# Buffers and products with v of an RWKV scan step, taken after the step before it

## The chip, the cores and the metric

One core of one Trainium2 chip. The time is the device time of one execution in microseconds (us); the kernel before was run three times. The trace is of one more execution, taken with the profiler.

## The reference, cut to what matters

A two-layer encoder on 256 tokens of width 1024. Each layer is a half feed-forward block, a mixer of three branches, and a second half feed-forward block; every block is scaled and shifted by rows that are products of the conditioning vector with `ada_w`. The mixer:

```python
o_a = dilated_attention(...); o_b = neighborhood_attention(...)
o_c = rwkv7_bidirectional(...)
merged = (sigmoid(gz0) * (o_a @ w_branch[0]) + sigmoid(gz1) * (o_b @ w_branch[1])
          + sigmoid(gz2) * (o_c @ w_branch[2]))
return merged @ w_out
```

and in `rwkv7_bidirectional`, over 256 tokens, 8 heads of 64, two directions:

```python
sa = einsum("dbhvk,dbhk->dbhv", state, a_vec)
state = state * w[..., None, :] + sa[..., None] * b_vec[..., None, :] + v[..., None] * k[..., None, :]
y = einsum("dbhvk,dbhk->dbhv", state, r)
```

## The kernel before, in words

**Dense work.** Weights are read once, in order, in tiles of 128x1024 f32 (`wraw`), split into a high part on ScalarE (`whi`, L360) and a low part on VectorE (`wlo`, L369), and used on TensorE in threes of matmuls (L404 to L406), one three for each 128x128 weight tile. In what follows a "dense three" is such a three. Four split quarters and three raw tiles may be held at once. In a mixer the dense work is: projections for the scan, for attention A and B, then branch A with its gates, the gates of branch C (tile `sg2`, two buffers), branch B with its gates, and at last branch C, whose input `oC` is what the scan leaves; then `w_out`.

**The scan in chunks.** The 256 steps of the recurrence are four chunks of 64 tokens, for both directions at once (chunk n of the one direction with chunk 3-n of the other). `invert` makes for a chunk the products `pG` (tile G, two buffers, L1161), a first inverse of 8x8 blocks (`blocks8`: many small VectorE steps on `w`, one TensorE product with `b8`), and three rounds of `pX`, a copy, `pT`, a masked copy into `TT` and a transpose (`flip`, L1245). There are two such threads, for chunks 0 and 2 and for 1 and 3. `values` makes the transposes `pBT` (tile `bu`), the product `pvt` of v (tile `uv`) and `pMV` (tile `W1`), and runs beside the three rounds. `scan` goes through the four chunks one after another: `pAS` added to W1, `pU`, the new state `pS1`, the output `pY`. `post` then normalises (`pvar`, `pgi`) and leaves `oC`.

**Buffers.** Most tiles lie in 34 equal buffers (`big`; semaphore `s_big`). `invert` takes at its start all that a chunk needs: two for G, one each for `uv`, `bu` and `tw` (and one for `tx` per thread), and no more than two chunks may hold theirs (`s_ck`). The scan gives them back when it has ended the chunk. The loads of `ada_w` (`araw`, 512 KB each, 72 a layer, L495; each used by one VectorE instruction, L468) take a buffer each from the same 34, and so do the gates `sg2` and much of attention.

**Order.** All of it is written by threads of Python generators. A planner (`Order`) gives each step an estimated duration, keeps a clock for each engine, and lets the thread go on that can start first; what comes out is the order of the instructions in each engine's queue. On the chip each queue runs in that order, and an instruction that waits holds all behind it in its queue. So a thread that may start earlier or later in the plan moves instructions in all queues.

Of the kernel before, what the change touches and what calls it, by code (L numbers as in the profile page):

```python
# [24 lines left out]
NBIG, NZ, NZ2 = 34, 10, 2  # L25
NRAW, NSPL, NADA, NPM = 3, 4, 2, 3
ORDER = "cabAgB"
NCK, NLR = 2, 2
WARM = 0
NJ0 = 8  # L30
NXF, NXM = 4, 8
# [4 lines left out]
VPRIO = 4  # L36
# [125 lines left out]
def wait(ev):  # L162
    return ("wait", ev, 0, 0)
# [6 lines left out]
def take(sem, n=1):  # L170
    return ("take", sem, n, 0)
# [20 lines left out]
def trunk(ctx, tc, A, out):  # L192
# [9 lines left out]
    od = Order()  # L202
    s_raw, s_spl, s_ada = Sem(NRAW), Sem(NSPL), Sem(NADA)
    s_pm, s_px, s_big = Sem(NPM), Sem(8 - NPM), Sem(NBIG)
# [9 lines left out]
    def big(name, shape=(128, 4, S), dt=F32):  # L214
        return act.tile(list(shape), dt, name=name, tag="b4", bufs=NBIG)
# [7 lines left out]
    def free_big(n=1):  # L223
        od.release(s_big, n)
# [597 lines left out]
    def half(h):  # L822
        return slice(64 * (h % 2), 64 * (h % 2) + 64)
# [29 lines left out]
    def mixer(l, st):  # L853
# [268 lines left out]

        e_inv, e_val = ([Event() for _ in range(4)] for _ in range(2))
        CH = {}
        s_ck = Sem(NCK)
        n_inv, e_got = [0], [Event() for _ in range(5)]

        def toks(c):
            return slice(c * 64, c * 64 + 64)
# [1 line left out]
        def invert(ns):  # L1131
            for e in e_ab:
                yield wait(e)
            for n in ns:
                cs = (n, 3 - n)
                if n > 0:
                    yield wait(e_got[n - 1])
                yield take(s_ck)
                for _ in range(5 - (n == 3) + (n == ns[0])):
                    yield take(s_big)  # L1140
                od.set(e_got[n])
                if n == ns[0]:
                    tx = big("tx", (128, 2, 2, 4, 64))
                    T, X = tx[:, 0], tx[:, 1]
                G = [big("G", (128, 2, 4, 128)) for _ in range(2)]
                uv = big("uv", (128, 2, 8, 64))
                bu = big("bu", (128, 2, 8, 64)) if n < 3 else None
                tw = big("tw", (128, 2, 2, 4, 64))
                TT, W1 = tw[:, 0], tw[:, 1]
                for d in range(2):  # L1150
                    yield take(s_px, 2)
                    pp = [paux("pG", (128, 4, 128)) for _ in range(2)]
                    yield on("PE", 1.3)
                    for i in range(4):
                        for b in range(2):
                            hs = half(b)
                            P.matmul(pp[b][:, i], BK[d][i // 2][hs, i % 2, cs[d]].rearrange("p a b -> p (a b)"),
                                     ar_view(d, i // 2)[hs, :, i % 2, toks(cs[d])], start=True, stop=True)
                    for b in range(2):
                        yield on("DVE", 0.6)  # L1160
                        V.tensor_mul(G[b][:, d], pp[b], mg[:, d][:, None, :].to_broadcast([128, 4, 128]))  # L1161
                        od.release(s_px)
                yield from blocks8(G, X, TT)
                yield on("DVE", 0.6)
                flip(T, TT)
                od.spawn(values(n, cs, G, bu, uv, W1), VPRIO)
                for lv in range(3):
                    w = 8 << lv

                    def part_(t, d, a):  # L1170
                        return t[:, d].rearrange("p h c -> p (h c)").rearrange("p (x a s) -> p x a s", a=2, s=w)[:, :, a]

                    def halves_(t, a):
                        return skew(part_(t, 0, a), part_(t, 1, 1 - a))

                    yield take(s_px)
                    px = paux("pX", (128, 2, 4, 64))
                    yield on("PE", 0.85)
                    for d in range(2):
                        for h in range(8):  # L1180
                            P.matmul(px[half(h), d, h // 2], G[h % 2][half(h), d, h // 2, 0:64], T[half(h), d, h // 2],  # L1181
                                     start=True, stop=True)
                    if lv == 0:
                        yield from copy_any(X, px, 512)
                    else:
                        yield from copy_any(halves_(X, 0), halves_(px, 0), 256)
                    od.release(s_px)
                    yield take(s_px)
                    pt = paux("pT", (128, 2, 4, 64))
                    yield on("PE", 0.85)  # L1190
                    for d in range(2):
                        for h in range(8):
                            P.matmul(pt[half(h), d, h // 2], X[half(h), d, h // 2], TT[half(h), d, h // 2], start=True, stop=True)  # L1193
                    yield on("DVE", 0.335)
                    V.copy_predicated(halves_(TT, 1), lvl[:, lv].rearrange("p d (x s) -> p d x s", s=w), halves_(pt, 1))
                    od.release(s_px)
                    if lv < 2:
                        yield on("DVE", 0.6)
                        flip(T, TT)
                CH[n] = (G, bu, uv, TT, W1)  # L1200
                yield wait(e_val[n])
                od.set(e_inv[n])
            n_inv[0] += 1
            free_big(1 if n_inv[0] == 1 else 5)

        def blocks8(G, m, TT):

# [36 lines left out]

            V.transpose(t.rearrange("p d a b -> p (d a b)"), tt.rearrange("p d a b -> p (d a b)"))  # L1245

        def values(n, cs, G, bu, uv, W1):
            for d in range(2):
                yield wait(e_rkv[d, 2])
            if n < 3:  # L1250
                yield take(s_px, 2)
                p = [paux("pBT", (128, 2, 4, 64)) for _ in range(2)]
                yield on("PE", 0.9)
                for d in range(2):
                    for i in range(4):
                        for b in range(2):
                            hs = half(b)
                            P.transpose(p[b][:, d, i], BK[d][i // 2][hs, i % 2, cs[d]].rearrange("p a b -> p (a b)"), ident[hs, hs])
                for b in range(2):
                    yield from copy_any(bu[:, :, b:8:2], p[b], 512)  # L1260
                    od.release(s_px)
# [17 lines left out]
            yield from copy_any(W1, p, 512)  # L1279
            od.release(s_px)  # L1280
            od.set(e_val[n])

        e_y = {(d, t): Event() for d in range(2) for t in range(2)}

        def scan():
            ST = st2 = None
            yield wait(e_ab[0])
            yield take(s_big)
            for n in range(4):
                cs = (n, 3 - n)  # L1290
                yield wait(e_inv[n])
                G, bu, uv, TT, W1 = CH[n]
                ar = lambda d, h, z: ar_view(d, h // 4)[half(h), z, h // 2 % 2, toks(cs[d])]
                dh = [(d, h) for d in range(2) for h in range(8)]
                if ST is None:
                    st2 = big("st", (128, 2, 2, 4, 64))
# [49 lines left out]
                od.release(s_px)  # L1346
                free_big(5 - (n == 3))
                od.release(s_ck)
                ST = sn
            free_big(5)  # L1350

# [566 lines left out]
```

## Time and profile before

| | |
|---|---|
| median of three runs | 1579.02 us (1576.25 to 1579.44) |
| profiled execution | 1579.55 us, span of its trace 1577.7 us |
| PE (matmul) busy | 1509.2 us, 96% of the span |
| PEld (weight load) busy | 1440.4 us, 91% |
| DVE busy | 1288.8 us, 82% |
| ACT busy | 856.1 us, 54% |
| DMA, mean | 197 GB/s |

PE is the engine with the most work. The shares are over the whole program; the mixers of the two layers (about 210 to 615 us and 980 to 1385 us) are where it has stretches without work. The granted TensorE clock is 1.00 (2.4 GHz) nearly everywhere and 0.50 (1.2 GHz) in a few stretches of the mixers.

### The profile page before, as it was taken

The numbers are of one execution on the slowest core, as the hardware profiler recorded it, in microseconds if no ns is written. First come the engines' busy times: TensorE is split into PE (matmuls) and PEld (weight loads), VectorE is DVE, ScalarE is ACT, GpSimd is POOL, SyncE is SP. The second block draws the span as 40 slices with busy tenths as digits, with TensorE's granted clock in tenths as the row PEclk, the third lists the DMA queues.
The fourth block names the chain that finished last, engine by engine and source line by source line (L and its number), as shares of the span: only waits on it lengthen the run. The fifth ranks groups of instructions, "written<-read, shape, count | busy, mean of one in ns | idle before, by whom it ended". The sixth has DMA issues, their size and how long they took to land.

```text
span 1577.7 us, 36363 instructions
## 1 busy us (share of the span) xinstructions
PE 1509.2 (96%) x14470; PEld 1440.4 (91%) x14470; DVE 1288.8 (82%) x2732; ACT 856.1 (54%) x1730; POOL 2.3 (0%) x22
## 2 busy tenths in 40 slices
PE   6999999999899989999999999999999987999997
PEld 6998999979689879999999999998888977999997
DVE  8888789989768688988789877999897687998664
ACT  4556457566344347555565545676654433665554
POOL 0000000000000000000000000000000000000000
PEclk9999999999899969999999999999999988999999
DMA  9687864446223435887668885543652352457553
GB/s 345 215 301 269 277 224 162 163 147 234 100 95 133 135 139 196 274 289 262 221 208 278 276 273 195 189 159 129 219 165 100 122 190 106 146 202 267 188 187 121
DMA packets 96226, 311.58 MB, mean 197 GB/s; under 512 B 11444, under 2 KB 22964, under 8 KB 96056
## 3 DMA queue, kind: packets, MB, share of 16 engines
q1 hardware_dynamic: 95768, 309.15, 57.8%
q8 instruction: 113, 1.85, 0.5%
q14 instruction: 57, 0.47, 0.1%
q10 hardware_dynamic: 288, 0.10, 0.0%
HBM read 308.17 MB, written 1.05 MB: 196 GB/s over the span
## 4 chain that ended last, share of the span: by engine, by line
PE 88%; DVE 6%; DMA 3%; issue 1%; ACT 1%; SPq 1%; DVEq 0%; ACTq 0%
PE pmain L404 21%; PE pmain L405 20%; PE pmain L406 20%; DMA araw<-in_ada_w_dram 3%; PE pearly L404 2%; PE pearly L406 2%; PE pearly L405 2%; PE pX L1181 1%; DVE araw L468 1%; PE pT L1193 1%; PE pS L1499 1%; PE pfirst L405 1%; PE pfirst L406 1%; PE pfirst L404 1%; DVE wlo L369 1%
## 5 line engine op out<-in xcount | busy, mean ns | idle before, releaser
L360 ACT CAST whi<-wraw 128x512 fp32r<-128x512 f32 x828 | 508.5, 619 | 444.6 <-PE pmain L405 291.8
L369 DVE TENSOR_TENSOR wlo<-wraw,whi 128x512 fp32r<-128x512 f32 x828 | 566.6, 689 | 118.0 <-ACT whi L360 108.0
L404 PE MATMUL pmain<-h,whi 128*128 128x256 f32 x1840 | 528.1, 287 | 0.0
L405 PE MATMUL pmain<-h,whi 128*128 128x256 f32 x1840 | 517.4, 281 | 0.0
L406 PE MATMUL pmain<-h,wlo 128*128 128x256 f32 x1840 | 515.6, 280 | 0.0
L404 PEld LDWEIGHTS pmain<-h,whi 128*128 128x128 f32 x1840 | 346.1, 188 | 12.2 <-issue 8.2
L406 PEld LDWEIGHTS pmain<-h,wlo 128*128 128x128 f32 x1840 | 347.4, 189 | 0.3 <-DVE wlo L369 0.2
L405 PEld LDWEIGHTS pmain<-h,whi 128*128 128x128 f32 x1840 | 346.4, 188 | 1.1 <-issue 0.7
L468 DVE CUSTOM_DVE_ANT_0 araw<-araw,csb 128x1024 f32<-128x1024 f32 x144 | 174.7, 1218 | 47.1 <-DMA araw<-in_ada_w_dram 46.9
L406 PE MATMUL pmain<-z,wlo 128*128 128x256 f32 x704 | 198.5, 282 | 7.0 <-DVE wlo L369 7.0
L405 PE MATMUL pmain<-z,whi 128*128 128x256 f32 x704 | 198.4, 282 | 0.0
L404 PE MATMUL pmain<-z,whi 128*128 128x256 f32 x704 | 197.7, 281 | 0.0
L406 PEld LDWEIGHTS pmain<-z,wlo 128*128 128x128 f32 x704 | 132.8, 189 | 8.5 <-DVE wlo L369 8.4
L404 PEld LDWEIGHTS pmain<-z,whi 128*128 128x128 f32 x704 | 132.7, 189 | 0.0
L405 PEld LDWEIGHTS pmain<-z,whi 128*128 128x128 f32 x704 | 132.7, 188 | 0.0
L404 PE MATMUL pearly<-xh,whi 128*128 128x258 f32 x320 | 91.5, 286 | 0.0
L406 PE MATMUL pearly<-xh,wlo 128*128 128x258 f32 x320 | 90.4, 283 | 0.0
L405 PE MATMUL pearly<-xl,whi 128*128 128x258 f32 x320 | 90.1, 282 | 0.0
L405 PEld LDWEIGHTS pearly<-xl,whi 128*128 128x128 f32 x320 | 60.6, 189 | 0.0
L404 PEld LDWEIGHTS pearly<-xh,whi 128*128 128x128 f32 x320 | 60.6, 189 | 0.0
L406 PEld LDWEIGHTS pearly<-xh,wlo 128*128 128x128 f32 x320 | 60.4, 189 | 0.0
L427 ACT CAST z<-ffz 128x256 fp32r<-128x256 f32 x76 | 30.6, 405 | 35.2 <-DVE ffz L659 34.8
(301 smaller groups left out, 2369.8 us busy)
## 6 DMA issues: line engine op xcount, KB each, us to landing
wraw<-in_ffn_wi_dram SPq DMA_DIRECT2D x160, 512.0 KB, 4.6
araw<-in_ada_w_dram SPq DMA_DIRECT2D x144, 512.0 KB, 6.4
wraw<-in_ffn_wo_dram SPq DMA_DIRECT2D x88, 512.0 KB, 4.6
wraw<-in_w_in_dram SPq DMA_DIRECT2D x78, 512.0 KB, 4.0
wraw<-in_w_gb_dram SPq DMA_DIRECT2D x72, 512.0 KB, 3.8
w0raw<-in_ffn_wi_dram SPq DMA_DIRECT2D x16, 512.0 KB, 11.1
wraw<-in_w_out_dram SPq DMA_DIRECT2D x16, 512.0 KB, 3.7
bt<-in_bt_dram SPq DMA_DIRECT2D x16, 192.0 KB, 4.7
```

The costliest lines, as they stand in the source:

```text
L360: S_.copy(hi, part(q))
L369: V.tensor_tensor(lo, part(q), hi, op=OP.subtract)
L404: P.matmul(o, w[0], xh, start=first, stop=False)
L405: P.matmul(o, w[0], xl, start=False, stop=False)
L406: P.matmul(o, w[1], xh, start=False, stop=last)
L427: S_.copy(self.hi(k), src)
L468: V.tensor_tensor_reduce(out=raw, in0=raw, in1=csb, scale=0.5, scalar=0.0, op0=OP.mult, op1=OP.add, accum_out=modT[l][:, blk:blk + 1])
L1181: P.matmul(px[half(h), d, h // 2], G[h % 2][half(h), d, h // 2, 0:64], T[half(h), d, h // 2], start=True, stop=True)
L1193: P.matmul(pt[half(h), d, h // 2], X[half(h), d, h // 2], TT[half(h), d, h // 2], start=True, stop=True)
L1499: P.matmul(pS[e][:, t], qT[half(e), hp, t * 128:(t + 1) * 128], kT[half(e), hp], start=True, stop=True)
```

## The change

`invert` takes three buffers a chunk instead of five and no longer waits for `values` at its end. `values` takes `uv` and `bu` itself, in the order of the chunks, and only one chunk may hold them (`s_vl` is one): the scan gives it back when it has ended a chunk. So `pBT`, `pvt` and `pMV` of chunk n are made after the scan of chunk n-1, and the scan waits for both events.

```diff
@@ -25,7 +25,7 @@
 NBIG, NZ, NZ2 = 34, 10, 2
 NRAW, NSPL, NADA, NPM = 3, 4, 2, 3
 ORDER = "cabAgB"
-NCK, NLR = 2, 2
+NCK, NLR, NVL = 2, 2, 1
 WARM = 0
 NJ0 = 8
 NXF, NXM = 4, 8
@@ -1122,8 +1122,8 @@
 
         e_inv, e_val = ([Event() for _ in range(4)] for _ in range(2))
         CH = {}
-        s_ck = Sem(NCK)
-        n_inv, e_got = [0], [Event() for _ in range(5)]
+        s_ck, s_vl = Sem(NCK), Sem(NVL)
+        n_inv, n_val, e_got, e_vgot = [0], [0], *([Event() for _ in range(5)] for _ in range(2))
 
         def toks(c):
             return slice(c * 64, c * 64 + 64)
@@ -1136,15 +1136,13 @@
                 if n > 0:
                     yield wait(e_got[n - 1])
                 yield take(s_ck)
-                for _ in range(5 - (n == 3) + (n == ns[0])):
+                for _ in range(3 + (n == ns[0])):
                     yield take(s_big)
                 od.set(e_got[n])
                 if n == ns[0]:
                     tx = big("tx", (128, 2, 2, 4, 64))
                     T, X = tx[:, 0], tx[:, 1]
                 G = [big("G", (128, 2, 4, 128)) for _ in range(2)]
-                uv = big("uv", (128, 2, 8, 64))
-                bu = big("bu", (128, 2, 8, 64)) if n < 3 else None
                 tw = big("tw", (128, 2, 2, 4, 64))
                 TT, W1 = tw[:, 0], tw[:, 1]
                 for d in range(2):
@@ -1163,7 +1161,7 @@
                 yield from blocks8(G, X, TT)
                 yield on("DVE", 0.6)
                 flip(T, TT)
-                od.spawn(values(n, cs, G, bu, uv, W1), VPRIO)
+                od.spawn(values(n, cs, G, TT, W1), VPRIO)
                 for lv in range(3):
                     w = 8 << lv
 
@@ -1197,11 +1195,8 @@
                     if lv < 2:
                         yield on("DVE", 0.6)
                         flip(T, TT)
-                CH[n] = (G, bu, uv, TT, W1)
-                yield wait(e_val[n])
                 od.set(e_inv[n])
-            n_inv[0] += 1
-            free_big(1 if n_inv[0] == 1 else 5)
+            free_big()
 
         def blocks8(G, m, TT):
 
@@ -1244,9 +1239,18 @@
 
             V.transpose(t.rearrange("p d a b -> p (d a b)"), tt.rearrange("p d a b -> p (d a b)"))
 
-        def values(n, cs, G, bu, uv, W1):
+        def values(n, cs, G, TT, W1):
             for d in range(2):
                 yield wait(e_rkv[d, 2])
+            if n > 0:
+                yield wait(e_vgot[n - 1])
+            yield take(s_vl)
+            for _ in range(1 + (n < 3)):
+                yield take(s_big)
+            od.set(e_vgot[n])
+            uv = big("uv", (128, 2, 8, 64))
+            bu = big("bu", (128, 2, 8, 64)) if n < 3 else None
+            CH[n] = (G, bu, uv, TT, W1)
             if n < 3:
                 yield take(s_px, 2)
                 p = [paux("pBT", (128, 2, 4, 64)) for _ in range(2)]
@@ -1279,6 +1283,9 @@
             yield from copy_any(W1, p, 512)
             od.release(s_px)
             od.set(e_val[n])
+            n_val[0] += 1
+            if n_val[0] == 4:
+                free_big(4)
 
         e_y = {(d, t): Event() for d in range(2) for t in range(2)}
 
@@ -1288,6 +1295,7 @@
             yield take(s_big)
             for n in range(4):
                 cs = (n, 3 - n)
+                yield wait(e_val[n])
                 yield wait(e_inv[n])
                 G, bu, uv, TT, W1 = CH[n]
                 ar = lambda d, h, z: ar_view(d, h // 4)[half(h), z, h // 2 % 2, toks(cs[d])]
@@ -1346,6 +1354,7 @@
                 od.release(s_px)
                 free_big(5 - (n == 3))
                 od.release(s_ck)
+                od.release(s_vl)
                 ST = sn
             free_big(5)
 
```

What this does to the queues is shown at three places.

**TensorE where branch C begins, layer 0.** `o` is the output of attention B, `oC` that of the scan. Before:

```order
L404 MATMUL pmain<-o,whi 128x256
L405 MATMUL pmain<-o,whi 128x256
L406 MATMUL pmain<-o,wlo 128x256
L1337 MATMUL pY<-G,uv 64x64 x16
L1341 MATMUL pY<-ar,st 64x64 x16
L1302 MATMUL pAS<-st,ar 64x64 x16
L1310 MATMUL pU<-tw 64x64 x16
L1337 MATMUL pY<-G,uv 64x64 x16
L1341 MATMUL pY<-ar,st 64x64 x16
L1402 MATMUL pvar<-c_sel,gsq 128x2 x8
L1420 MATMUL pgi<-c_ident,gsq 128x128 x8
L404 MATMUL pmain<-oC,whi 128x256
```

With the change:

```order
L404 MATMUL pmain<-o,whi 128x256
L405 MATMUL pmain<-o,whi 128x256
L406 MATMUL pmain<-o,wlo 128x256
L404 MATMUL pmain<-oC,whi 128x256
L405 MATMUL pmain<-oC,whi 128x256
L406 MATMUL pmain<-oC,wlo 128x256
```

The scan's last steps no longer stand between the two: the last `pgi` of layer 0 is now 35 dense threes ahead of the end of branch B. In layer 1 the products that stood there (two whole inversions, two `pvt`, two `pMV`, two steps of the scan) are gone too but for one last `pgi` directly ahead of branch C; the last `pY` stands 26 dense threes ahead.

**VectorE in the first inversion, layer 0.** `w_` with a number is the small tile of one chunk's 8x8 blocks. Before, the second chunk's begins after the scan's first `uv` copy (L1312):

```order
L369 TENSOR_TENSOR wlo<-wraw,whi 128x512
L1195 COPY_PREDICATED tw<-lvl,pT 128x2x4x32
L1161 TENSOR_TENSOR G<-pG,c_mg 128x512 x2
L1312 COPY uv<-pU 64x8x64
L1161 TENSOR_TENSOR G<-pG,c_mg 128x512 x2
L1215 TENSOR_TENSOR tx<-G,c_m_112 64x512 x2
L1218 COPY w_5657<-c_d_113 128x64
L1219 TENSOR_REDUCE w_5657<-tx 128x64
```

With the change it runs between the steps of the first chunk's:

```order
L1228 TENSOR_TENSOR w_5233<-p_5288,w_5233 128x8x4
L1210 TENSOR_TENSOR tx<-G,c_m_112 64x512
L1232 TENSOR_TENSOR w_5233<-w_5233 128x2x4x4
L1210 TENSOR_TENSOR tx<-G,c_m_112 64x512
L1228 TENSOR_TENSOR w_5233<-p_5288,w_5233 128x8x3
L1213 COPY w_5334<-c_d_113 128x64
L1214 TENSOR_REDUCE w_5334<-tx 128x64
L1232 TENSOR_TENSOR w_5233<-w_5233 128x2x4x3
```

The 8x8 blocks of the second inversion have moved ahead of the 207th split `wlo` of the program, into the time in which branch A is done and the gates of branch C wait for buffers.

**The queue of loads (SP), end of the mixer of layer 1.** `w_gb` holds the gates and branches, `w_out` comes after branch C. Before:

```order
L495 DMA araw<-in_ada_w_dram 128x1024 x2
L345 DMA wraw<-in_w_gb_dram 128x1024 x5
L495 DMA araw<-in_ada_w_dram 128x1024
L345 DMA wraw<-in_w_out_dram 128x1024
L495 DMA araw<-in_ada_w_dram 128x1024 x12
L345 DMA wraw<-in_w_out_dram 128x1024 x7
```

With the change:

```order
L495 DMA araw<-in_ada_w_dram 128x1024 x2
L345 DMA wraw<-in_w_gb_dram 128x1024
L495 DMA araw<-in_ada_w_dram 128x1024
L345 DMA wraw<-in_w_gb_dram 128x1024 x2
L495 DMA araw<-in_ada_w_dram 128x1024 x2
L345 DMA wraw<-in_w_gb_dram 128x1024 x8
L345 DMA wraw<-in_w_out_dram 128x1024 x8
```

The twelve `ada_w` loads that were behind the first `w_out` tile have moved ahead of the last eight `w_gb` tiles. In layer 0 eight moved likewise, and eight now follow each other where three did, near the first inversion.

## Rows read from the trace of the kernel before

**Rows 1.** The page's part 1, TensorE's line alone.

```profile
PE 1509.2 (96%) x14470; PEld 1440.4 (91%) x14470; DVE 1288.8 (82%) x2732; ACT 856.1 (54%) x1730; POOL 2.3 (0%) x22
```

**Rows 2.** Busy time by stretch, layer 0: stall, interleaved part, tail, and slow-clock parts.

```profile
core 0: us, PE busy (x) PEld busy (x) DVE busy (x) ACT busy (x) POOL busy (x), PEclk, DMA share, GB/s
401.10:445.20 44.10, 35.18 (x504) 28.13 (x504) 33.42 (x86) 15.70 (x40) 0.00 (x0) 0.88 0.25 83
405.80:416.03 10.23, 8.98 (x32) 5.89 (x34) 8.76 (x32) 1.68 (x3) 0.00 (x0) 0.50 0.53 198
445.20:544.70 99.50, 99.14 (x1596) 93.00 (x1594) 71.83 (x158) 44.90 (x85) 0.00 (x0) 1.00 0.37 123
544.70:576.46 31.76, 21.05 (x245) 18.84 (x244) 23.10 (x51) 8.35 (x18) 0.00 (x0) 0.62 0.40 150
552.57:576.46 23.89, 16.54 (x114) 14.81 (x115) 18.12 (x41) 7.08 (x15) 0.00 (x0) 0.50 0.32 130
```

**Rows 3.** The same view, layer 1: stall, interleaved part, tail, and slow-clock parts.

```profile
1176.40:1195.70 19.30, 14.89 (x386) 13.40 (x385) 11.57 (x20) 5.32 (x10) 0.00 (x0) 1.00 0.44 146
1195.70:1290.80 95.10, 94.19 (x1094) 86.58 (x1092) 72.46 (x159) 46.12 (x99) 0.00 (x0) 1.00 0.37 123
1291.00:1347.87 56.87, 41.72 (x864) 36.97 (x864) 43.45 (x104) 15.56 (x32) 0.00 (x0) 0.79 0.37 140
1293.26:1303.50 10.24, 7.10 (x96) 5.32 (x98) 9.57 (x30) 1.66 (x3) 0.00 (x0) 0.50 1.01 381
1330.81:1334.22 3.41, 3.22 (x54) 3.10 (x56) 0.00 (x0) 0.14 (x1) 0.00 (x0) 0.50 0.00 0
1337.64:1347.87 10.23, 7.86 (x31) 6.63 (x32) 7.32 (x20) 3.21 (x9) 0.00 (x0) 0.50 0.01 2
```

**Rows 4.** Timeline, tail of layer 0: start us, duration us, what [idle before <-releaser].

```profile
546.63 5.35 SPq L495 DMA_DIRECT2D araw<-in_ada_w_dram  x8
...
569.71 0.58 PE L404 MATMUL pmain<-oC,whi 128*128 128x256 f32 x1 [3.73 <-ACT oC L1447]
```

**Rows 5.** Timeline, stall of layer 0.

```profile
401.95 0.69 DVE L369 TENSOR_TENSOR wlo<-wraw,whi 128x512 fp32r<-128x512 f32 x1
...
407.05 2.08 PE L1228 MATMUL p<-tx,c_b 128*128 128x512 f32 x2 [5.21 <-DVE tx L1222]
...
409.16 0.22 DVE L1233 TENSOR_TENSOR w<-p,w 128x56 f32<-128x56 f32 x1 [0.49 <-PE p L1228]
...
415.83 0.17 DVE L1237 TENSOR_TENSOR w<-w 128x8 f32<-128x8 f32 x1
...
432.30 0.69 DVE L369 TENSOR_TENSOR wlo<-wraw,whi 128x512 fp32r<-128x512 f32 x1 [2.71 <-ACT whi L360]
```

**Rows 6.** Groups of instructions by line on VectorE: busy us, mean ns | idle before.

```profile
L468 DVE CUSTOM_DVE_ANT_0 araw<-araw,csb 128x1024 f32<-128x1024 f32 x144 | 174.7, 1218 | 47.1 <-DMA araw<-in_ada_w_dram 46.9
...
L1161 DVE TENSOR_TENSOR G<-pG,c_mg 128x512 f32<-128x512 f32 x32 | 21.1, 683 | 2.8 <-PE pG L1157 2.7
...
L1245 DVE STREAM_TRANSPOSE tx<-tw 128x512 f32<-128x512 f32 x24 | 16.9, 707 | 0.3
L1215 DVE TENSOR_TENSOR tx<-G,c_m 64x512 f32<-64x512 f32 x16 | 10.9, 682 | 0.2
L1219 DVE TENSOR_REDUCE w<-tx 128x64 f32<-128x512 f32 x8 | 9.2, 1151 | 0.0
```

**Rows 7.** Busy time by stretch where two inversions run at once, end of layer 1's mixer.

```profile
1280.00:1320.00 40.00, 30.42 (x580) 27.06 (x578) 38.17 (x92) 11.56 (x21) 0.00 (x0) 0.87 0.65 238
```

**Rows 8.** Answer for the tile araw from 380 to 620 us: its loads.

```profile
DMA to landing us min/median/max: 4.9/6.2/8.1
```

**Rows 9.** Answers for the tiles pvt, pMV and pBT: copies of their results (ns min/median/max).

```profile
L849 ACT COPY uv<-pvt x16: 578/580/582, 428.5 to 1321.9; 64x512 f32<-64x512 f32 x16
...
L849 ACT COPY tw<-pMV x8: 585/586/588, 430.9 to 1326.9; 128x512 f32<-128x512 f32 x8
...
L849 ACT COPY bu<-pBT x12: 585/589/595, 419.9 to 1302.0; 128x512 f32<-128x512 f32 x12
```

**Rows 10.** The chain that ended last, 450 to 500 us: products at the full clock.

```profile
456.56 0.65 PE pBT L1258 x16
...
470.15 1.08 PE pAS L1302 x32
...
481.98 1.09 PE pG L1157 x16
```

## The prediction

> **What bounds the kernel now.** I read the page's busy shares first. TensorE (PE) is busy 96% of the span [rows 1], and the change neither adds nor removes a matmul, so it can only give back time in which PE has nothing to do or runs at half clock. For that I cut the mixers by the view of busy time by stretch, at the points where PE's queue goes from dense threes to other work and back. What a stretch loses I count as its length, less PE's busy time, plus half of what PE did while the granted clock stood at 0.50, that is at 1.2 GHz where 2.4 is the full rate. The reader should see six numbers.
>
> Layer 0 [rows 2]: the stall after branch A loses 44.10 - 35.18 + 8.98/2 = 13.4 us; the interleaved part up to the end of branch B loses 0.4; the tail loses 31.76 - 21.05 + 16.54/2 = 19.0. Layer 1 [rows 3]: the stall loses 4.4, the interleaved part 0.9, the tail 56.87 - 41.72 + (7.10 + 3.22 + 7.86)/2 = 24.2. Together 62.3 us, of which the two tails are 43.2.
>
> In a tail the dense work that needs no scan has run out, and branch C waits: the timeline has its first matmul at 569.71, released by the copy to oC [rows 4]. The tail is the scan's chain, alone. The stall of layer 0 is another thing: PE waits there for VectorE (5.21 us at 407.05 for the blocks' tx) [rows 5], which is busy 33.42 of 44.10 us [rows 2]. So VectorE, with its dependences, is what a longer stall would be made of.
>
> **The change, part by part.** The instructions stay the same in kind and number; each term is a move.
>
> *The tails.* In the changed order the last pgi of layer 0 stands 35 dense threes ahead of the end of branch B. I take the tail of layer 0 as gone: -19.0 us, half-clock start of branch C included, since PE comes to it busy. In layer 1 the last pgi stands directly ahead of branch C, so what follows it remains: two VectorE products, the copy to oC and the low part. The row that is nearest is the 3.73 us that PE waited for just that chain in layer 0 [rows 4], at half clock and with one ada instruction in between. I take 3, with ends 0 and 8 (twice the row, if VectorE is behind). So layer 1 gives 24.2 - 3 = 21.2.
>
> *Stall of layer 0.* Between the 206th and 207th split (401.95 to 432.30) [rows 5] VectorE's queue gets the second chunk's start: four G, two tx, one reduction, 14 small steps of about 0.2, a transpose and three more ada instructions, against a few attention and bonus steps that move behind. By their durations [rows 5, 6] that is 4 x 0.68 + 2 x 0.68 + 1.15 + 14 x 0.2 + 0.71 + 3 x 1.22 = 12.4, less about 3: some 10 us more VectorE work, while PE gets 4.6 more work in the stretch (two pG of 1.09, a block product of about 1, one more pX and pT of 1.08, less what moved out; [rows 5, 10]). VectorE would then need 33.4 + 10 = 43.4 us. At its present share, 76%, that is 57 us against a PE work of 44.1 - 13.4 + 4.6 = 35.3: 22 lost. At 100%: 8 lost. The nearest row is the end of layer 1's mixer, where two inversions do run at once: VectorE is busy 38.17 of 40 us there, 95% [rows 7]. At 90% the stretch takes 48 and loses 13. I take no change, with ends -5 and +9.
>
> In the same place eight ada loads now follow each other in SP's queue, some behind buffers that VectorE or the last attention product gives back. A load takes 6.2 us to land, up to 8.1 [rows 8]; VectorE comes to the one that is issued last about 5 us after its buffer is free, so it waits 1 us or 2, inside the ends above. The w_gb tile behind them in SP's queue is for the 211th split, more than 10 us of VectorE's work later, so it hides. The Trainium skill, DMA: Bandwidth & Descriptors, Anatomy of one DMA, gives 2.0 us plus bytes over 436 GB/s, measured for loads that GpSimd issues; for 512 KB my estimate from it is 3.2 us, and the sum would be better by the 1 or 2 us; the trace's 6.2 differs from it and decides.
>
> *Interleaved part of layer 0.* From the 206th to the 222nd split VectorE's queue goes from about 48 to about 80 us: ten more ada, eight G, four tx, two reductions, some twenty small steps, three transposes, and the first post steps, by their durations [rows 5, 6] about 32 us. PE's work up to the same dense threes goes from about 60 to about 80. So two full queues with dependences between them stand where PE lost 0.4 us before. Here the change puts values on the scan's path: for each later chunk pvt (1.08, as the like product has), two copies of 0.58, pMV, a copy of 0.59 [rows 9, 10], ahead of them pBT of 0.65 and two copies. PE cannot pass them; what covers them is dense threes (two to five between each, 0.7 to 1.8 us) and the other inversion. If the cover is right they cost nothing, and if not each gap is lost at once. I take +5, ends 0 and +12.
>
> *Stall of layer 1.* VectorE gets about 13 us more between its splits, PE 7.5 us more; attention B's second half now lies in it. PE's work is 14.9 + 7.5 = 22.4; VectorE's 11.6 + 13 = 24.6, at 90% 27 us, and its attention chain adds some: +4, ends 0 and +10. The clock stayed at 1.00 through this stall [rows 3], and fell to 0.50 in that of layer 0 [rows 2]; were it to fall here as there, the price is half of 8.98 us, and the upper end holds it. The Trainium skill, TensorE: Matmul & The Clock Gate, HAM oscillation, says that waits for operands throw the clock back again and again; by it this fall would come and the sum would be about 4 us worse, and the trace shows it in one of two stalls.
>
> *Interleaved part of layer 1.* As in layer 0 but with less moved (VectorE 38 to 67, PE to 73 us): +3, ends 0 and +8.
>
> *The sum.* -19.0 - 21.2 + 0 + 5 + 4 + 3 = -28.2. The profiled execution took 1579.55 us (span 1577.7): 1551.3. It lies 0.5 above the median of the runs, so I say **1551 us**. Nothing outside the mixers changes its order.
>
> **The rivals.**
>
> *Full cover.* The two inversions fill each other's waits and the values are hidden: nothing is paid but 3 us of layer 1's tail, and the stall of layer 0 wins 3: about 1536. For it: 0.4 and 0.9 lost where scan and dense work are interleaved now [rows 2, 3]. Against it: VectorE has 72 of 99 us busy there, and gets more. Chance 0.2.
>
> *VectorE becomes the bound early.* The stall of layer 0 goes at 76% (+9), the interleaved parts and the stall of layer 1 near their upper ends (+8, +6, +4): -40 + 27 = -13, about 1566. For it: the 5.21 us wait [rows 5]. Against: the 95% where two inversions run [rows 7]. Chance 0.18.
>
> *Slower: the scan's path becomes the bound.* In six scan steps values now stand between one step and the next. Each is 1.08 + 0.58 + 0.58 + 1.08 + 0.59 = 3.9 us, four of them with 1.8 more for bu: 31 us [rows 9, 10]. If PE, which runs its queue in order, waits through all of it, and the stalls and interleaved parts go to half of their upper ends beside it (+20), the sum is -40 + 31 + 20 = +11: about 1590. It decides from the point where a scan step loses over 5 us on average. Against it: before, pAS and pU stood in the same stream and 0.4 us was lost. Chance 0.08.
>
> *No change.* The tails come back at the same length elsewhere, since the scan ends no earlier on the chip than now: within 3 us of 1579. The order speaks against it: nothing of the scan stands behind branch B. Chance 0.04.
>
> **How the numbers follow.** The forecast, 1543 to 1559, has 0.5. From no change a measurement here can tell about 0.2%, 3 us. Faster by more: 0.5 + 0.2 + 0.18 = 0.88; the same 0.04; slower 0.08. A range from 1535 to 1568 takes in the first three cases but for their edges, and leaves out some 0.2.
>
> **What would show it.** Right: after the last branch B matmul branch C begins within 4 us in both layers, at clock 1.00; oC no longer ends a wait of 3.7 us in layer 0; the stretch after branch A still loses 10 to 17 us in layer 0; some 30 us of ada and inversion work on VectorE stand earlier. Wrong: PE waits of over 2 us before pMV, pAS or pU (scan's path), VectorE over 90% busy with PE idle through the gates of branch C, or a tail that remains.

## The result, and the profile after

The changed kernel took 1559.12 us, median of four runs (1555.30 to 1562.21), against 1578.42 for the kernel before on the same chip; ratio 0.9878, 95% interval [0.9853, 0.9904]. The prediction was 1551, with 1535 to 1568 as its range; the narrower band of 1543 to 1559 was just missed. Two later comparisons gave the same kernel 0.9845 [0.9827, 0.9863] and 0.9851 [0.9832, 0.9871], so the gain is 19 to 26 us where 28.2 were forecast. The profiled execution took 1555.30 us, span 1553.5, which is 24.2 less than the span shown of before; the terms below are held against that pair.

Part 1 of the page after, beside [rows 1]:

```profile
PE 1509.0 (97%) x14470; PEld 1439.7 (93%) x14470; DVE 1283.1 (83%) x2724; ACT 869.1 (56%) x1744; POOL 2.3 (0%) x22
```

TensorE's instructions are the same, in a shorter span; VectorE has eight fewer and ScalarE 14 more, with 13 us more to do there. Busy time by stretch, layer 0: the stall after branch A, its two pieces at 0.50, the interleaved part, and the first of branch C; columns as in [rows 2].

```profile
400.90:450.00 49.10, 40.14 (x662) 33.09 (x660) 40.08 (x107) 17.30 (x43) 0.00 (x0) 0.86 0.48 150
404.70:414.94 10.24, 8.35 (x38) 5.89 (x38) 9.26 (x27) 1.83 (x5) 0.00 (x0) 0.50 0.52 176
421.77:425.18 3.41, 3.34 (x40) 3.20 (x40) 3.41 (x10) 1.47 (x5) 0.00 (x0) 0.50 0.29 64
450.00:556.50 106.50, 106.50 (x1655) 98.88 (x1654) 81.77 (x174) 52.65 (x101) 0.00 (x0) 1.00 0.35 116
556.50:567.80 11.30, 11.30 (x98) 11.30 (x97) 10.80 (x25) 6.79 (x13) 0.00 (x0) 1.00 0.58 190
```

By the prediction's count (length, less PE's busy time, plus half of what PE did at 0.50) the stall loses 49.10 - 40.14 + (8.35 + 3.34)/2 = 14.8, and the rest nothing: the tail of 19.0 [rows 2] is gone, and branch C starts at the full clock. The longest wait in the stall is again the one for the blocks' tx. The profile names no releaser for it, but VectorE's instruction that makes this tx (L1217) ends 0.1 us before the product (L1223) starts:

```profile
405.81 0.68 DVE L1217 TENSOR_TENSOR tx<-w,c_d 128x512 f32<-128x512 f32 x1
...
406.59 2.04 PE L1223 MATMUL p<-tx,c_b 128*128 128x512 f32 x2 [4.29 <-issue]
```

Where the tail went is seen at the third chunk. Before, its first pG began at 482.0 us [rows 10], 42 us after the first chunk's last products (pY) had begun:

```profile
439.59 1.15 PE L1337 MATMUL pY<-G,uv 128*64 128x64 f32 x32
```

With the change, 2.5 us lie between the two:

```profile
450.20 1.15 PE L1345 MATMUL pY<-G,uv 128*64 128x64 f32 x32
...
452.69 1.16 PE L1155 MATMUL pG<-ar,bk 64*128 64x128 f32 x16
```

Layer 1, beside [rows 3], in the same order:

```profile
1161.60:1196.60 35.00, 28.39 (x458) 22.76 (x457) 27.61 (x77) 10.73 (x30) 0.00 (x0) 0.85 0.35 117
1165.88:1172.70 6.82, 6.82 (x76) 4.86 (x72) 5.22 (x12) 0.59 (x1) 0.00 (x0) 0.50 0.40 134
1179.53:1182.94 3.41, 3.27 (x64) 3.08 (x60) 3.34 (x13) 1.71 (x9) 0.00 (x0) 0.50 0.47 141
1196.60:1312.90 116.30, 115.81 (x1828) 106.92 (x1828) 87.91 (x180) 57.89 (x107) 0.00 (x0) 1.00 0.42 142
1312.90:1331.40 18.50, 15.04 (x102) 14.14 (x102) 15.33 (x39) 9.38 (x20) 0.00 (x0) 0.82 0.36 115
1316.06:1322.89 6.83, 5.38 (x22) 4.92 (x23) 4.94 (x13) 1.77 (x4) 0.00 (x0) 0.50 0.26 80
```

The stall loses 6.6 + 5.05 = 11.7 where it lost 4.4, the interleaved part 0.5, the start of branch C 3.46 + 2.7 = 6.1 in place of 24.2. What ends the last wait is seen in the timeline of TensorE, layer 0 (two rows) and layer 1 (three):

```profile
556.52 0.28 PE L406 MATMUL pmain<-o,wlo 128*128 128x256 f32 x1
556.64 0.28 PE L404 MATMUL pmain<-oC,whi 128*128 128x256 f32 x1
...
1313.07 0.60 PE L1429 MATMUL pgi<-c_ident,gsq 128*128 128x128 f32 x4
1315.32 0.39 PE L404 MATMUL pmain<-oC,whi 128*128 128x256 f32 x1 [1.66 <-ACT oC L1456]
1317.18 0.58 PE L405 MATMUL pmain<-oC,whi 128*128 128x256 f32 x1 [1.47 <-DVE oC L1458]
```

In layer 0 branch C follows branch B in 0.12 us, where PE waited 3.73 [rows 4]. In layer 1 the last pgi still stands straight ahead of it and PE waits 1.66 and 1.47 for `oC`; then the clock is at 0.50 for the first of branch C.

### The profile page after: what moved, and what is told of

Its sections match the earlier page's. It is cut to its first block, busy times and chain, and to the rows that moved or that the text cites. A ratio compares the mean times of both kernels' runs of the same rounds, so it can differ in the third digit from the quotient of the medians.

```text
span 1553.5 us, 36369 instructions
## 1 busy us (share of the span) xinstructions
PE 1509.0 (97%) x14470; PEld 1439.7 (93%) x14470; DVE 1283.1 (83%) x2724; ACT 869.1 (56%) x1744; POOL 2.3 (0%) x22
## 4 chain that ended last, share of the span: by engine, by line
PE 90%; DVE 5%; DMA 2%; issue 1%; ACT 1%; SPq 0%; DVEq 0%; ACTq 0%
PE pmain L404 22%; PE pmain L405 21%; PE pmain L406 20%; PE pearly L404 3%; PE pearly L406 2%; PE pearly L405 2%; PE pT L1191 1%; DMA araw<-in_ada_w_dram 1%; PE pX L1179 1%; PE pG L1155 1%; PE pfirst L405 1%; PE pfirst L406 1%; PE pmain L1664 1%; PE pfirst L404 1%; PE pmain L1666 1%
## 5 line engine op out<-in xcount | busy, mean ns | idle before, releaser
L427 ACT CAST z<-ffz 128x256 fp32r<-128x256 f32 x76 | 30.6, 405 | 29.5 <-DVE ffz L659 28.2
## 6 DMA issues: line engine op xcount, KB each, us to landing
w0raw<-in_ffn_wi_dram SPq DMA_DIRECT2D x16, 512.0 KB, 11.1
```

What stands on the lines that cost most here:

```text
L427: S_.copy(self.hi(k), src)
```

## The experiments

The table gives what each run's profile lost, in us, counted as above between the same dense threes of the program. "Inner" is from the stall to the end of branch B, "end" the last wait and the start of branch C.

| kernel | stall 0 | inner 0 | end 0 | stall 1 | inner 1 | end 1 | sum | median us | ratio to before |
|---|---|---|---|---|---|---|---|---|---|
| before | 13.4 | 0.4 | 19.0 | 4.4 | 0.9 | 24.2 | 62.3 | 1578.4 | |
| changed | 14.8 | 0 | 0 | 11.7 | 0.5 | 6.1 | 33.1 | 1559.1 | 0.9878 |
| changed again (e1) | 15.6 | 0 | 0 | 8.7 | 0.5 | 6.1 | 30.9 | 1553.9 | 0.9845 |
| changed again (e11) | 16.0 | 0 | 0 | 8.8 | 0.5 | 6.3 | 31.6 | 1556.1 | 0.9851 |
| two chunks' values (e2) | 15.2 | 0.1 | 1.1 | 10.3 | 0.1 | 6.6 | 33.4 | 1553.6 | 0.9840 |
| gates one by one (e3) | 12.6 | 0.3 | 4.5 | 11.1 | 0.1 | 7.0 | 35.6 | 1558.5 | 0.9877 |
| before, gates one by one (e4) | 15.8 | 14.4 | 0 | 7.5 | 21.4 | 0 | 59.1 | 1575.5 | 0.9976 |
| two buffers fewer (e5) | 16.1 | 1.7 | 23.9 | 18.9 | 6.1 | 41.2 | 107.9 | 1625.2 | 1.0287 |
| one inversion (e6) | 0.9 | 0.1 | 64.4 | 0 | 0 | 48.0 | 113.4 | 1629.2 | 1.0308 |
| before, one buffer more (e7) | 13.5 | 0 | 9.7 | 7.4 | 27.6 | 0 | 58.2 | 1593.0 | 1.0086 |
| ada loads earlier (e8) | 20.8 | 0 | 4.2 | 14.7 | 2.4 | 0 | 42.1 | 1560.9 | 0.9874 |
| ada loads later, layer 0 (e9) | 4.8 | 0.7 | 7.4 | 8.7 | 2.2 | 7.3 | 31.1 | 1556.1 | 0.9859 |
| e9's idea and e3's (e10) | 10.2 | 0 | 7.6 | 11.9 | 0.1 | 6.8 | 36.6 | 1560.2 | 0.9880 |
| later in 0, earlier in 1 (e12) | 12.4 | 0.3 | 4.8 | 13.2 | 1.9 | 4.1 | 36.7 | 1561.4 | 0.9883 |

**The changed kernel again (e1, e11), no edit.**

> The changed kernel once more, for comparison on the same chip as the next three. Both theories: ratio to before 0.985 to 0.990 (1555 to 1562 us).

> The changed kernel once more on the chip of the two others. 1553 to 1561 us, layer 0's stall loses 14 to 16 us.

Measured 1553.93 (1553.32 to 1556.44), ratio 0.9845, a little better than expected, and 1556.08 (1553.35 to 1557.84). The order is the same and the losses nearly so; what differs is where the clock falls. The stall of layer 1 in e1, and its one piece at 0.50:

```profile
1162.70:1195.30 32.60, 25.57 (x459) 20.43 (x458) 27.57 (x77) 10.72 (x30) 0.00 (x0) 0.95 0.37 125
...
1167.90:1171.30 3.40, 3.40 (x37) 2.42 (x35) 3.37 (x7) 0.26 (x1) 0.00 (x0) 0.50 0.37 125
```

With 3.4 us at half clock instead of 10.2 the stretch is 2.4 us shorter. TensorE is busy 2.8 us less in it and waits 0.4 more; VectorE's busy time is the same, 27.6.

**Two chunks may hold their values (e2).**

```diff
-NCK, NLR, NVL = 2, 2, 1
+NCK, NLR, NVL = 2, 2, 2
```

> The changed kernel, but two chunks instead of one may hold the buffers of the values; the inversion still takes three buffers. Theory A (the gain comes from the two buffers that an inversion no longer needs to start, so that the second inversion runs beside the first): the same order in the main, no tail, 1555 to 1565 us. Rival B (the gain comes from making the values only after the preceding scan step, which spreads the work): most of it is lost, 1570 to 1580 us.

Measured 1553.56 (1551.46 to 1555.94), ratio 0.9840 [0.9821, 0.9859]: no different from e1 on the same chip, and a little under theory A's range. That only one chunk may hold its values plays no part in the gain.

The edit hardly moves the values, so it is a weak test of rival B. The traces say more. In layer 0 of the kernel before, the products pvt of the second to fourth chunk begin at 459.2, 518.9 and 531.2 us, and the pY of the chunk ahead of each at 439.6, 478.8 and 544.9: two of three stood behind it already. Over both layers it is four of six before, four in e2 and all six with the change. So the change moves few of these products, and their place can be little of the gain.

**The freed buffers taken back (e5).**

```diff
-NBIG, NZ, NZ2 = 34, 10, 2
+NBIG, NZ, NZ2 = 32, 10, 2
```

> The changed kernel with 32 big buffers instead of 34: the two that an inversion no longer takes are out of the pool. Theory A (buffers): the third chunk's products come after the dense work again, the tails are back in both layers, the gain is gone or worse, 1580 to 1640 us. Rival B (the gain comes from where the values are made): values still stand behind the preceding scan step, so most of the gain stays, 1555 to 1568 us.

Measured 1625.19, ratio 1.0287 [1.0261, 1.0313]: both tails are back, longer than before. The last stretch of layer 0 and of layer 1:

```profile
545.00:598.20 53.20, 39.19 (x571) 36.25 (x570) 37.25 (x84) 16.26 (x33) 0.00 (x0) 0.78 0.37 134
1297.20:1402.70 105.50, 82.46 (x1447) 73.28 (x1446) 74.88 (x164) 30.65 (x62) 0.00 (x0) 0.79 0.31 106
```

The values are made late here too, so their place alone gives no gain, and rival B falls. But the tail of layer 0 did not come back in the way theory A says: the third chunk's pG stands nearly as close behind the scan as in the changed kernel (2.9 us). What comes late is pBT, the first of the values of the second chunk, which `values` makes when it has its two buffers:

```profile
458.12 1.16 PE L1155 MATMUL pG<-ar,bk 64*128 64x128 f32 x16
...
500.53 0.71 PE L1262 MATMUL pBT<-c_ident,bk 64*128 64x64 f32 x16
```

In the changed kernel this pBT stands at 454.7. In layer 1 of e5 even the first chunk's pBT waits until branch B is done (1297.5). So e5 shows that the gain hangs on two buffers in the pool, not that an inversion's take is what needs them.

**One inversion at a time (e6).**

```diff
-NCK, NLR, NVL = 2, 2, 1
+NCK, NLR, NVL = 1, 2, 1
```

> The changed kernel with one chunk in flight instead of two (an inversion starts only when the scan has given back the chunk before). Theory A (the gain is the second inversion running beside the first): both tails come back longer than before, 1610 to 1680 us, but the stall in layer 1 shrinks to 5 us lost or less. Rival B (the two inversions need not overlap): within 10 us of the changed kernel, 1545 to 1565 us.

Measured 1629.21, ratio 1.0308 [1.0277, 1.0338]. Theory A, and its second half as well: with one inversion in flight the stalls are all but gone (0.9 and 0), and the tails are enormous:

```profile
488.90:617.00 128.10, 85.17 (x1462) 75.83 (x1461) 65.11 (x147) 27.93 (x58) 0.00 (x0) 0.76 0.10 36
1307.40:1405.50 98.10, 63.99 (x1031) 55.97 (x1030) 54.54 (x126) 22.48 (x47) 0.00 (x0) 0.77 0.09 29
```

So the same work makes stall and tail: two inversions side by side at the end of branch A, or their chain after branch B. The two do not cost the same; here the tails alone lose 112 us, and in the changed kernel all six places 33.

**The kernel before, with buffers got in other ways (e4, e7).** In e4 `gates2` takes its two buffers when each is needed, in e7 there is one big buffer more.

```diff
-            yield take(s_big, 2)
-            sg2 = [big("sg2") for _ in range(2)]
+            sg2 = []
...
+                if m % 4 == 0:
+                    yield take(s_big)
+                    sg2.append(big("sg2"))
```

```diff
-NBIG, NZ, NZ2 = 34, 10, 2
+NBIG, NZ, NZ2 = 35, 6, 2
```

> The kernel before, with that one edit alone (the gates of branch C take their two buffers one at a time): invert still takes five buffers and waits for the values. In its order the last post step of layer 0 stands 60 dense threes ahead of branch C and that of layer 1 48 ahead. Theory A (buffers decide; the change under study is one way among others to get the second inversion started early): both tails are gone without the change, 20 to 40 us faster than before, 1540 to 1560 us. Rival B (the values must move behind the scan for that): the scan steps wait for values and inversions, and the time stays within 8 us of before, 1571 to 1587 us.

> The kernel before with 35 big buffers instead of 34, room for which is made by 6 instead of 10 small ones; values as before. In its order the last post step of layer 1 stands 58 dense threes ahead of branch C, that of layer 0 still behind branch B. Theory A (buffers): the tail of layer 1 is gone and its stall is longer, the tail of layer 0 stays, 1555 to 1570 us. Rival B (the values' place decides): 1574 to 1590 us.

e4 measured 1575.53, ratio 0.9976 [0.9961, 0.9991]; e7 1593.03, ratio 1.0086 [1.0057, 1.0114]. Both are misses for theory A as it stood; e4's time lies in rival B's range, e7's 3 us above it. The tails went where the order said (both in e4, layer 1's in e7), and the time did not follow. Branch C of layer 1 in e4 loses nothing, and the stretch ahead of it does, as in e7 (one row of each kernel):

```profile
1196.70:1279.20 82.50, 69.63 (x1078) 60.13 (x1077) 61.92 (x150) 30.49 (x69) 0.00 (x0) 0.88 0.23 73
...
1340.30:1351.70 11.40, 11.40 (x99) 11.40 (x98) 10.85 (x25) 6.80 (x13) 0.00 (x0) 1.00 0.54 185
```

```profile
1205.70:1292.90 87.20, 70.39 (x1150) 60.88 (x1149) 64.54 (x147) 26.09 (x57) 0.00 (x0) 0.88 0.30 109
```

Rival B's mechanism, scan steps that wait for values, is not seen there. In e4 TensorE waits for the inversions' tx (waits by line: us, times, longest):

```profile
PE p L1228 <- DVE tx L1222: 7.0, 2, 4.2
PE pX L1181 <- DVE tx L1245: 4.9, 3, 4.2
```

Only 42 dense threes, 15 us of work, stand in that stretch of either kernel, with most of three inversions. In e7 the products pG of the second, third and fourth chunk of layer 1 begin within 30 dense threes. In the changed kernel 73 dense threes lie between the first and the last of these, and nothing of this kind is lost. So an earlier start of the inversions isn't enough for a gain. That they must come at a pace at which inversions and dense threes can be mixed, which the change happens to give, is read from these orders; no run changes the pace alone. e7 also lost 13.2 us between the mixers (3.3 before). Its four fewer small buffers are the likely reason, though no run separates them, so its time says little of the mixers.

**The gates one by one in the changed kernel (e3).** The first edit of e4, in the changed kernel.

> The changed kernel, but the gates of branch C take their two buffers one at a time, each when its first gate needs it. Theory A2 (the stall after branch A is the dense list standing at the take of two buffers, and in layer 1 it grew from 5 to 12 us lost since the second inversion now takes the freed buffers first): the stalls of 15.5 and 12.4 us lost shrink by 10 to 18 us together, 1538 to 1550 us. Rival B2 (the stall is made of VectorE's work for two inversions): the same waits for the blocks' tx stand a little later, within 4 us of the changed kernel, 1552 to 1564 us.

Measured 1558.54, ratio 0.9877 [0.9856, 0.9897], 5 us behind e1. This is rival B2: the gates no longer wait for two buffers at once, and the stalls still lose 12.6 and 11.1. Stall of layer 0, with VectorE busy for 40.90 of 45.70:

```profile
400.40:446.10 45.70, 36.33 (x625) 29.34 (x625) 40.90 (x109) 16.26 (x40) 0.00 (x0) 0.93 0.47 161
```

**The ada loads moved (e8, e9, e12).** The loads start 110 us after the mixer in the plan's clock; the edits change that. e8:

```diff
-            od.spawn(ada([(l, 5), (l, 7), (l, 6)], 9, PACE, START), 9)
+            od.spawn(ada([(l, 5), (l, 7), (l, 6)], 9, PACE, 60 if l == 0 else 80), 9)
```

> The changed kernel with the ada loads of a mixer started at 60 us of the plan in layer 0 and 80 in layer 1 instead of 110: none of the ada steps of layer 0 stands between the 206th and the 222nd split any more, and the last post step of layer 1 stands 50 dense threes ahead of branch C. Theory C (the stall after branch A lasts as long as VectorE's queue in it, ada steps of 1.22 us among it): layer 0's stall loses 3 to 6 us less, layer 1's tail 6 us less, 1540 to 1550 us. Rival D (the stall is the chain of one inversion's dependent steps, whatever else VectorE does): the stall of layer 0 loses 13 to 16 as now, only the tail's 6 us go, 1547 to 1554 us.

Measured 1560.92, ratio 0.9874 [0.9842, 0.9906]. The text misjudged its own order: the trace has eleven ada steps in layer 0's stall, where the changed kernel has nine. The stall grew, to 20.8 lost. It is no test between C and D as written. The tail of layer 1 did go (6.1 to 0), and its stall and inner part lost 17.1 together, where the changed kernel lost 9.2 to 12.2.

e9:

```diff
-            od.spawn(ada([(l, 5), (l, 7), (l, 6)], 9, PACE, START), 9)
+            od.spawn(ada([(l, 5), (l, 7), (l, 6)], 9, PACE, 150 if l == 0 else START), 9)
```

> The changed kernel with the ada loads of layer 0's mixer started at 150 us of the plan instead of 110 (layer 1 as it was). In its order one ada step stands between the first tx and the sixth transpose of layer 0's inversions, where the changed kernel has eight. Theory C (the stall after branch A lasts as long as VectorE's queue in it): 7 x 1.22 = 8.5 us less VectorE work there, the stall of layer 0 loses 5 to 9 us less than its 15; the last pgi of layer 0 comes just ahead of branch C, which gives 3 to 5 back; 1550 to 1556 us, ratio 0.980 to 0.984. Rival D (the stall is the chain of the inversion's dependent steps): it loses 13 to 16 as now, 1556 to 1565 us.

Measured 1556.07 (1553.32 to 1561.90), ratio 0.9859, and 1556.08 for e11 on the same chip: no gain, and a ratio above theory C's. The stall of layer 0 by stretch:

```profile
405.80:442.60 36.80, 32.00 (x578) 27.18 (x576) 28.43 (x75) 16.43 (x42) 0.00 (x0) 1.00 0.40 126
```

Its ada steps, in the groups by line (busy us, mean ns | idle before), first e9, then the changed kernel:

```profile
L468 DVE CUSTOM_DVE_ANT_0 araw<-araw,csb 128x1024 f32<-128x1024 f32 x4 | 4.9, 1216 | 0.0
```

```profile
L468 DVE CUSTOM_DVE_ANT_0 araw<-araw,csb 128x1024 f32<-128x1024 f32 x9 | 10.8, 1204 | 0.0
```

The stall loses 4.8 instead of 16.0, and the clock stays at 1.00. That is against rival D, and more than theory C had. It is a gain of 11.2, of which the end of layer 0 takes back 7.4, since its last pgi now stands straight ahead of branch C:

```profile
551.05 1.07 PE L1429 MATMUL pgi<-c_ident,gsq 128*128 128x128 f32 x8 [0.33 <-DVE gsq L1424]
...
556.23 0.58 PE L404 MATMUL pmain<-oC,whi 128*128 128x256 f32 x1 [4.11 <-ACT oC L1456]
```

and the other stretches 3.3 more. e9 has not only fewer ada steps there: both inversions also begin before the stall in it. The number of ada steps alone does not set the loss: in e2 five of them stand in this stretch, where e1 on the same chip has nine, and it loses 15.2 against 15.6.

```profile
L468 DVE CUSTOM_DVE_ANT_0 araw<-araw,csb 128x1024 f32<-128x1024 f32 x5 | 6.0, 1215 | 0.0
```

That leaves the earlier start of the second inversion as the likelier reason; no run moves it alone.

e12:

```diff
-            od.spawn(ada([(l, 5), (l, 7), (l, 6)], 9, PACE, START), 9)
+            od.spawn(ada([(l, 5), (l, 7), (l, 6)], 9, PACE, 130 if l == 0 else 90), 9)
```

> The changed kernel with the ada loads of layer 0's mixer started at 130 us of the plan and those of layer 1's at 90, instead of 110 in both. In its order the last pgi of layer 0 stands 2 dense threes ahead of branch C, that of layer 1 ten (in the changed kernel 35 and none); two ada steps instead of eight stand between the first tx and the sixth transpose of layer 0. Theory C (VectorE's queue sets the stall, and a last pgi a few dense threes ahead hides the tail): stall 0 loses 5 to 8, tail 0 up to 4, stall 1 9 to 11, tail 1 up to 1: 18 to 24 lost instead of 32, 1543 to 1550 us. Rival D (what leaves one place comes back in the next, as with the later ada loads alone): 1553 to 1561 us.

Measured 1561.40, ratio 0.9883 [0.9864, 0.9902]: rival D's outcome, just above its range. Five ada steps stand in layer 0's stall, but the second inversion begins inside it again, and it loses 12.4; layer 1's stall went from 8.8 to 13.2.

**e3 and later ada loads together (e10).** e3's edit, and

```diff
-            od.spawn(ada([(l, 5), (l, 7), (l, 6)], 9, PACE, START), 9)
+            od.spawn(ada([(l, 5), (l, 7), (l, 6)], 9, PACE, 130 if l == 0 else 110), 9)
```

> The changed kernel with both: the gates of branch C take their two buffers one at a time, and layer 0's ada loads start at 130 us of the plan. Theory C: with the ada steps out of it, PE gets dense threes into the stall of layer 0, which loses 5 to 8 us; 1546 to 1554 us. Rival D: no better than the gates alone were, 1555 to 1562 us.

Measured 1560.17, ratio 0.9880 [0.9861, 0.9899]: no better than e3. The stall of layer 0 loses 10.2, more than theory C's 5 to 8: four ada steps stand in it, as in e9, but the second inversion begins inside it. No version here beats the changed kernel.

## Why the prediction was right

*Tails.* Layer 0: -19.0 forecast, -19.0 measured. Layer 1: -21.2 forecast, 24.2 - 6.1 = -18.1 measured. The step that was short is the 3 us that were to remain of the chain behind the last pgi: its waits are 3.5 us by the row of the stretch (18.50 - 15.04), and half of 5.38 us at 0.50 was left out. The working had seen a half-clock start in layer 0 only as something that goes away. Of its signs, branch C within 4 us of branch B held in both layers (0.1 and 2.4), and the clock of 1.00 in layer 0 alone.

*Stall of layer 0.* 0 forecast, +1.4 measured (+2.2 and +2.6 in e1 and e11). VectorE was to need 43.4 us and be 90% busy, 48 us long and 13 lost; it did 40.08, was 82% busy, and the stretch is 49.10 long with 14.8 lost. These are two errors that cancel, so the near hit is luck.

*Stall of layer 1.* +4 forecast, +7.3 measured here, +4.3 and +4.4 in e1 and e11. PE's work was to be 22.4, and is 28.39 - 5.05 = 23.3 at the full clock. VectorE was to have 24.6 us of work and be 90% busy; it had 27.61 and was 79% busy. The share is the step that failed in both stalls. [rows 7] gave 95% at one place, and it did not carry over. Why it was so high there is open: 25 dense threes stood in those 40 us, nearly all ahead of 1290.5, and VectorE was busy 96% before that point and 95% after. TensorE waits for VectorE in this stall too, but for the tx and w ahead of pX and not, as in layer 0, for the blocks' tx (waits by line: us, times, longest):

```profile
PE pX L1179 <- DVE tx L1240: 4.0, 2, 2.7
PE pX L1179 <- DVE w L1228: 1.4, 1, 1.4
```

The clock fell here, for 10.2 us in the profile and 3.4 in e1; before, it had stayed at 1.00 [rows 3]. The Trainium skill, TensorE: Matmul & The Clock Gate, HAM oscillation, had it fall where the engine waits for operands, and the trace agrees: a wait of 2.7 us ends at 1165.27, and the clock falls at 1165.88. But before, with waits of up to 2.4 us in this stall, it did not fall. The price by the count is 5.0 us, 3.4 more than e1's 1.7; the stretch was 2.4 longer than e1's.

*Interleaved parts.* +5 and +3 were forecast as waits, and no wait came: 0 and 0.5 lost, against 0.4 and 0.9. The values stand on the scan's path, and dense threes and the other inversion cover them: the longest wait ahead of pMV, pAS or pU is 0.28 us. The slower rival's condition, 5 us lost in a scan step, was nowhere near. A cost of nearly that size came in another form. PE's busy time at the full clock is 1509.2 - 43.7/2 = 1487.4 before [rows 1 to 3] and 1509.0 - 30.6/2 = 1493.7 after (27.2 of the 30.6 in the rows above, 3.4 near 157 us): the same matmuls took 6.3 us more. By the same count e1 and e11 have 1490.5 and 1490.9, 3.1 and 3.5 more than before. The last section has the reason for about that much.

*The sum.* -19.0 - 18.1 + 1.4 + 7.3 - 0.4 - 0.4 in the mixers is -29.2; other stretches gave 1.3, and 6.3 went to the longer busy time: -24.2, the difference of the spans. The forecast of -28.2 was that of the losses, and that it came so near to -29.2 is luck: tails and stalls came out 3.1 + 1.4 + 3.3 = 7.8 worse than forecast, and the interleaved parts 8.8 better. What the sum lacked was a term for mixing itself. The mechanism of the main term is right: the tails are gone, but for 6.1 us.

*What was not seen.* That the change works through the overlap of inversions (e6) and needs the buffers (e5) was taken as given; that an earlier start alone is not enough (e4, e7) was not thought of. The prediction's sentence on VectorE, that a longer stall would be made of it, holds as a tendency and gives no length. In the stall of layer 0, VectorE's busy time and the length were 28.43 of 36.80 (e9), 33.42 of 44.10 [rows 2], 40.08 of 49.10 (changed), 40.90 of 45.70 (e3) and 37.84 of 50.80 (e2): 74 to 89%, while PE lost 4.8 to 15.2. PE's own share there is 79 to 87%, so neither engine was full, and each waited for the other. In the stretches that e4 and e7 lost it is 75 and 74%. The loads behind each other in SP's queue cost little: from 380 to 620 us VectorE waited for an ada load once, 2.9 us, where before it waited twice, 3.0 in all, and the loads landed in 5.0 us, median, against 6.2 [rows 8]; the estimate of 3.2 us, from the Trainium skill, DMA: Bandwidth & Descriptors, Anatomy of one DMA, stays below both. Open is which part of the change sets the pace of the inversions, what sets the paces of e4 and e12 apart from the changed kernel's, and the 7 us by which runs of the changed kernel differ, of which the clock's falls in different places are one part.

## What to carry to other kernels

When a chain of dependent work is started earlier so that dense work can cover it, look at the engine that makes the chain in the stretch where it lands, and give the length as a range. The share that this engine reaches does not carry from one stretch to another: VectorE's was 76 and 60% in the two stalls before [rows 2, 3], 82 and 79% with the change, and 95% where two inversions ran at the end of a mixer [rows 7]. What is won at one place can be lost at the next (e9 won 11.2 us and lost 10.7 again), so count losses over all stretches of a stage. A freed buffer is an earlier start for someone: find who takes it first, and who starves when it is missing (e5).

## What had not been expected

Changing between dense threes and other products costs TensorE time in which it counts as busy. The timeline of the changed kernel, going out of the dense threes and coming back:

```profile
1161.48 0.29 PE L405 MATMUL pmain<-o,whi 128*128 128x256 f32 x1
1161.61 0.28 PE L406 MATMUL pmain<-o,wlo 128*128 128x256 f32 x1
1161.82 0.39 PE L843 MATMUL pbon<-rowh,bsel 64*128 64x256 f32 x1
...
1195.95 0.39 PE L404 MATMUL pmain<-h,whi 128*128 128x256 f32 x1
1196.17 0.28 PE L405 MATMUL pmain<-h,whi 128*128 128x256 f32 x1
1196.29 0.28 PE L406 MATMUL pmain<-h,wlo 128*128 128x256 f32 x1
```

From one dense matmul to the next it is 0.12 us; from the last of them to another product 0.21, and from the first after such a product to the second 0.22. An excursion of this kind costs some 0.19 us beside its own work. The trace before has 138 excursions and that of the changed kernel 157, so an estimate is 19 x 0.19 = 3.6 of the 6.3 us above. The other 2.7 are no more than the three traces of the changed kernel differ among themselves (1490.5 to 1493.7).

The step outwards depends on how much of the array the next product takes, which the rows give as rows*columns (64*128 for pbon above). At the full clock, in the trace of the changed kernel, its median is 0.21 us where that is 64 rows, or 64 or 32 columns, and 0.12, as inside the dense work, where it is 128*128 or 65*128. There are 106 steps of the first kind, against 85 before, and 46 of the second, against 47. So what the change added are excursions of the dear kind. Why a part of the array costs this is not shown.

The granted clock is no fixed property of an order: the same program had 10.2 us at 0.50 in the stall of layer 1 in one profiled execution and 3.4 in two others.
